# Half of the modulated, transposed features leave PSUM through VectorE

## The chip, the cores and the metric

The kernel runs on one core of one Trainium2 chip. Its time is the device time of one execution in microseconds (us). A core has a matrix engine (TensorE, PE in the profile, with its weight loads as PEld), VectorE (DVE), ScalarE (ACT), GpSimd (POOL) and SyncE (SP), which issues most of the DMAs. Each engine works through its own queue in order, and the engines wait for each other by semaphores.

## The reference, cut to what matters

One step of a two-layer network runs on 128 context tokens and 256 latent tokens, 1024 features wide, in float32. In each layer a token-mixing part and a SwiGLU part are each entered through a normalisation and a modulation:

```python
def rms_norm(x, g):
    xf = x.astype(jnp.float32)
    y = xf * lax.rsqrt(jnp.mean(xf * xf, axis=-1, keepdims=True) + EPS)
    return (y * g.astype(jnp.float32)).astype(x.dtype)

def modulate(h, shift, scale):
    return h * (1 + scale) + shift

h = modulate(rms_norm(x, g_norm_l[0]), sh1, sc1)      # enters the token mixers
x = x + ga1 * rms_norm(mix, g_norm_l[1])
f = swiglu(modulate(rms_norm(x, g_norm_l[2]), sh2, sc2), w_gu_l, w_down_l)
x = x + ga2 * rms_norm(f, g_norm_l[3])
```

So between a residual update and the next matrix products each token's features are divided by their root mean square, multiplied by one number per feature and shifted by another.

## The kernel before, in words

The 384 tokens are three tiles of 128 (tile 0 context, tiles 1 and 2 latent). `x` holds tokens on partitions. The matrix products want the features on partitions, and every float32 product is done as three products of a high and a low part (`mm3`, L107), so the normalised rows must be transposed, modulated and split into a high part `hT[0]` and a low part `hT[1]`.

`norm_T` (L345) does this for one tile and one half `kh` of the features (four blocks of 128). TensorE transposes the four blocks into one PSUM tile `trp` (L350). ScalarE evicts each block with one activation, `scale * in + bias` with the per-feature columns `Amod` and `Bmod` (L355), into the SBUF tile `xm` (`u`). VectorE then casts `xm` to the high part (L359) and subtracts to get the low part (L360). There are three tiles and two halves, and three places where this function is used, 18 calls in all:

- the token mixers of layer 0, for the feed-forward part of layer 0: tiles 0 and 1 at the schedule's steps `00`, `10`, `01`, `11` (first digit the half, second the tile), tile 2 by `tail` inside `gu_first` (L1238);
- the end of the feed-forward part of layer 0, for the mixers of layer 1: `turn` (L1337) for tile 0, and for tiles 1 and 2 the list `tails`, which `tok_first` (L536) puts between its matrix products;
- the token mixers of layer 1, as in layer 0.

The first normalisation of layer 0 has code of its own (`hT_q`, L479) and is not touched.

The order of the work around these calls is fixed by hand. `SCHEDULE` (L22) is a list of step names for each layer, and the steps are traced inside `tc.manual_schedule(engines=ENGINES)`, under which TensorE, VectorE and ScalarE keep exactly the traced order; the two blocks of the feed-forward part that contain `tail` and `turn` are traced in the same way. The end of the list of layer 0 reads:

```python
"... q1b b2 y1 10 v13 A2 A1 01 A3 b2 b2 11 A4 A3 A1 r2a A2 g2a r2b g2b x2a x2b q2a A2 A1 q2b A1 y2 A3"
```

Layer 1 has there `q1b y1 b2 10 v13 01 b2 b2 A3 11 A2 r2a g2a A1 r2b x2a g2b x2b q2a A4 q2b y2`. Here `y1` and `y2` scale the rows of tiles 1 and 2 by their reciprocal root mean square (VectorE, L1171); `v13` is the last attention product and its eviction (L667, L668); `A` steps cast weights into high and low parts (ScalarE L118, VectorE L119); `b2` are the output projection's products of tile 2 and the addition of the two partial sums (VectorE, L749); `r2`, `g2`, `x2`, `q2` are, for tile 2, the sum of squares of the projection, its product with the gate (L1166), the residual update (L1168) and the sum of squares of the new `x` (ScalarE L321 to L326, VectorE L323). After `y2` the tile's rows `xn` go to `tail`.

In the end of the feed-forward part, `post` (L330) is the residual update of a tile (L333, L335), `norm_x` (L337) its normalisation (L311, L139, L140, L342), `next_w` casts weights of the next layer (L118, L119).

`norm_T` returns the last instruction that evicts and the last that subtracts. `gu_first` hands both to `tc.issue_after`, which queues what is traced later behind the given instruction, on that instruction's engine.

Of the kernel before, what the change touches and what calls it, by code (L numbers as in the profile page):

```python
# [11 lines left out]
AF = mybir.ActivationFunctionType  # L12
ALU = mybir.AluOpType
# [39 lines left out]
def hybrid_step(  # L53
# [8 lines left out]
    V, A, PE, G, SP = nc.vector, nc.scalar, nc.tensor, nc.gpsimd, nc.sync  # L62
# [37 lines left out]
    Amod = cp.tile([128, 2, 2, 2, 8], F32, name="Amod")  # L100
    Bmod = cp.tile([128, 2, 2, 2, 8], F32, name="Bmod")
# [243 lines left out]
    def norm_T(l, which, i, hT, t, kh, ps):  # L345
        s = 0 if i == 0 else 1
        u = tp.tile([128, 512], F32, tag="g2", name="xm", bufs=4)
        for k4 in range(4):
            k = 4 * kh + k4
            PE.transpose(ps[:, k4 * 128:(k4 + 1) * 128], t[:, k * 128:(k + 1) * 128], ident)  # L350
        for k4 in range(4):
            k = 4 * kh + k4
            dst = u[:, k4 * 128:(k4 + 1) * 128]
            src = ps[:, k4 * 128:(k4 + 1) * 128]
            a = A.activation(dst, src, AF.Identity, scale=Amod[:, l, which, s, k:k + 1],  # L355
                             bias=Bmod[:, l, which, s, k:k + 1])
        uv = u.rearrange("p (k t) -> p k t", k=4)
        hv = hT[0][:, kh * 4:(kh + 1) * 4, i * 128:(i + 1) * 128]
        V.tensor_copy(hv, uv)  # L359
        v = V.tensor_tensor(hT[1][:, kh * 4:(kh + 1) * 4, i * 128:(i + 1) * 128], uv, hv.bitcast(F32), ALU.subtract)  # L360
        return a.ins, v.ins
# [7 lines left out]
    def mixers(l, ma, mp, mn, pp, banks, h1T, steps, pairs, tails):  # L369
# [718 lines left out]
        def tile_T(i, t, pool, tag, khs=(0, 1)):  # L1088
            if not h2T:
                h2T.extend(new_hT())  # L1090
            for kh in khs:
                r = norm_T(l, 1, i, h2T, t, kh, pool.tile([128, 512], F32, tag=tag, name="trp"))
            return r
# [88 lines left out]
    def ffn(l, fa, fb, pp, steps, h2T, first, tail):  # L1182
# [154 lines left out]
        def turn(i, kh):  # L1337
            def f(pool, tag):
                if i not in xn:
                    xn[i] = norm_x(i)  # L1340
                norm_T(l + 1, 0, i, nh, xn[i], kh, pool.tile([128, 512], F32, tag=tag, name="trp"))
            return f
# [137 lines left out]
```

## Time and profile before

| | us |
|---|---|
| median of 3 runs | 1000.54 (1000.4 to 1001.1) |
| the profiled execution | 1001.41 |
| its span, from first to last instruction | 999.6 |
| TensorE busy | 966.1 (97%) |
| VectorE busy | 623.3 (62%) |
| ScalarE busy | 466.8 (47%) |

Times inside the trace are counted from the start of the span. The calls of `norm_T` lie at 217 to 245 (layer 0), 515 to 535 (between the layers) and 699 to 726 (layer 1).

```profile
PE   5999999999999999999999999999999999999997
PEclk8999999999999999999999999999999999999999
```

These two lines of the page cut the span into 40 slices of 25 us. The first gives TensorE's busy share in tenths, the second the clock granted to it in tenths of full speed: TensorE is nearly always busy, and in every slice but the first at 90% of full clock or more.

### The profile page before, as it was taken

The numbers are of one execution on the slowest core, as the hardware profiler recorded it, in microseconds if no ns is written. First come the engines' busy times: TensorE is split into PE (matmuls) and PEld (weight loads), VectorE is DVE, ScalarE is ACT, GpSimd is POOL, SyncE is SP. The second block draws the span as 40 slices with busy tenths as digits, with TensorE's granted clock in tenths as the row PEclk, the third lists the DMA queues.
The fourth block names the chain that finished last, engine by engine and source line by source line (L and its number), as shares of the span: only waits on it lengthen the run. The fifth ranks groups of instructions, "written<-read, shape, count | busy, mean of one in ns | idle before, by whom it ended". The sixth has DMA issues, their size and how long they took to land.

```text
span 999.6 us, 16493 instructions
## 1 busy us (share of the span) xinstructions
PE 966.1 (97%) x6537; PEld 838.9 (84%) x6537; DVE 623.3 (62%) x1036; ACT 466.8 (47%) x930; POOL 85.8 (9%) x142
## 2 busy tenths in 40 slices
PE   5999999999999999999999999999999999999997
PEld 3789886668999999999987898766899999999996
DVE  3566657767964979986265757677787533333323
ACT  4545537678533433333266346577873323333322
POOL 0312320000000200000010343000000000000000
PEclk8999999999999999999999999999999999999999
DMA  9958678407873777763033794430575344333001
GB/s 327 314 175 255 207 211 237 150 1 253 277 231 126 265 256 236 252 229 110 22 100 107 189 283 122 110 106 1 191 270 192 127 149 148 127 127 127 22 1 64
DMA packets 128414, 167.30 MB, mean 167 GB/s; under 512 B 15600, under 2 KB 90080, under 8 KB 128336
## 3 DMA queue, kind: packets, MB, share of 16 engines
q1 hardware_dynamic: 122112, 154.00, 48.2%
q0 software_dynamic: 5856, 12.09, 4.4%
q8 instruction: 51, 0.84, 0.4%
q14 instruction: 27, 0.22, 0.1%
q10 hardware_dynamic: 368, 0.16, 0.1%
HBM read 163.51 MB, written 2.70 MB: 166 GB/s over the span
## 4 chain that ended last, share of the span: by engine, by line
PE 84%; ACT 5%; DVE 4%; DMA 3%; issue 2%; SPq 1%; POOL 0%; ACTq 0%; DVEq 0%; POOLq 0%
PE gups L108 11%; PE gups L110 11%; PE gups L109 11%; PE facc L108 6%; PE facc L110 6%; PE facc L109 6%; PE tps L108 3%; PE fps L108 2%; PE tps L110 2%; PE tps L109 2%; PE fps L110 2%; PE fps L109 2%; PE ops L108 2%; PE adap L214 2%; PE ptp L1031 2%
## 5 line engine op out<-in xcount | busy, mean ns | idle before, releaser
L119 DVE TENSOR_TENSOR lo<-raw,hi 128x1024 fp32r<-128x1024 f32 x98 | 119.1, 1221 | 65.9 <-ACT hi L118 62.4
L118 ACT ACTIVATE hi<-raw 128x1024 fp32r<-128x1024 f32 x98 | 103.2, 1058 | 93.5 <-PE facc L110 86.9
L108 PE MATMUL gups<-hT,ring 128*128 128x384 f32 x416 | 141.1, 339 | 0.0
L110 PE MATMUL gups<-hT,ring 128*128 128x384 f32 x416 | 140.6, 338 | 0.0
L109 PE MATMUL gups<-hT,ring 128*128 128x384 f32 x416 | 140.4, 338 | 0.0
L179 DVE SCALAR_TENSOR_TENSOR spare<-araw,scol,spare 128x512 f32<-128x512 f32 x168 | 115.6, 745 | 4.5 <-DMA araw<-in_w_ada_dram 4.5
L108 PE MATMUL facc<-hi,f 128*128 128x512 f32 x240 | 95.8, 399 | 0.0
L110 PE MATMUL facc<-hi,f 128*128 128x512 f32 x240 | 94.7, 394 | 0.0
L109 PE MATMUL facc<-lo,f 128*128 128x512 f32 x240 | 94.6, 394 | 0.0
L108 PEld LDWEIGHTS gups<-hT,ring 128*128 128x128 f32 x416 | 78.1, 188 | 0.9 <-issue 0.2
L109 PEld LDWEIGHTS gups<-hT,ring 128*128 128x128 f32 x416 | 78.1, 188 | 0.3
L110 PEld LDWEIGHTS gups<-hT,ring 128*128 128x128 f32 x416 | 78.1, 188 | 0.0
L108 PE MATMUL gups<-hT,xring 128*128 128x384 f32 x224 | 76.0, 339 | 0.0
L110 PE MATMUL gups<-hT,xring 128*128 128x384 f32 x224 | 75.7, 338 | 0.0
L109 PE MATMUL gups<-hT,xring 128*128 128x384 f32 x224 | 75.6, 338 | 0.0
L108 PE MATMUL tps<-hi,hT 128*128 128x512 f32 (+1 forms) x192 | 68.5, 357 | 2.6 <-DVE hT L486 2.6
L110 PE MATMUL tps<-hi,hT 128*128 128x512 f32 (+1 forms) x192 | 65.2, 339 | 0.0
L109 PE MATMUL tps<-lo,hT 128*128 128x512 f32 (+1 forms) x192 | 65.1, 339 | 0.0
L1209 ACT ACTIVATE ring<-spare 128x1024 fp32r<-128x1024 f32 x26 | 27.6, 1060 | 61.3 <-PE gups L109 35.5
L1209 ACT ACTIVATE ring<-rgu 128x1024 fp32r<-128x1024 f32 x26 | 27.6, 1061 | 60.3 <-PE gups L109 35.4
L1224 DVE TENSOR_TENSOR sg<-sg,gups 128x384 f32<-128x384 f32 x40 | 22.1, 552 | 53.7 <-PE gups L110 53.7
L108 PEld LDWEIGHTS facc<-hi,f 128*128 128x128 f32 x240 | 45.1, 188 | 11.2 <-issue 1.8
(304 smaller groups left out, 2018.2 us busy)
## 6 DMA issues: line engine op xcount, KB each, us to landing
araw<-in_w_ada_dram SPq DMA_DIRECT2D x80, 512.0 KB, 4.8
raw<-in_w_down_dram SPq DMA_DIRECT2D x44, 512.0 KB, 4.6
raw<-in_w_in_dram SPq DMA_DIRECT2D x40, 512.0 KB, 5.9
spare<-in_w_gu_dram SPq DMA_DIRECT2D x20, 1024.0 KB, 5.2
rgu<-in_w_gu_dram SPq DMA_DIRECT2D x20, 1024.0 KB, 5.7
sraw<-in_w_ada_dram SPq DMA_DIRECT2D x16, 512.0 KB, 9.8
raw<-in_w_out_dram SPq DMA_DIRECT2D x8, 512.0 KB, 6.3
G<-row POOLq DMA_DIRECT2D x8, 512.0 KB, 6.1
```

What stands on the lines that cost most here:

```text
L108: PE.matmul(out, lhsT=wh, rhs=xh, start=start, stop=False)
L109: PE.matmul(out, lhsT=wh, rhs=xl, start=False, stop=False)
L110: PE.matmul(out, lhsT=wl, rhs=xh, start=False, stop=stop)
L118: a = A.activation(hi[:, :n], raw, AF.Copy)
L119: v = V.tensor_tensor(lo[:, :n], raw, hi[:, :n].bitcast(F32), ALU.subtract)
L179: V.scalar_tensor_tensor(acc[:, s], raw[:, k2], scol[:, k, s:s + 1], acc[:, s], ALU.mult, ALU.add)
L214: PE.matmul(ps[32 * g:32 * g + 32], lhsT=scol[:, 2 * kk + k2], rhs=raw[:, k2, g * 128:(g + 1) * 128], start=k2 == 0, stop=k2 == 1)
L1031: PE.transpose(pt[:, hd, b * 128:(b + 1) * 128], self.P[:, hd, b * 128:(b + 1) * 128], ident)
L1209: A.activation(hi, rv, AF.Copy)
L1224: V.tensor_tensor(sg, sg, pu, ALU.mult)
```

## The change

In `norm_T` the eviction of the second half (`kh` = 1) of each tile is done by VectorE: one multiplication of all four blocks by the column `Amod`, repeated along the tokens by a broadcast view, from PSUM into `xm`, and one addition of `Bmod`, broadcast likewise, in place. The first half stays on ScalarE. The cast and the subtraction follow as before. The instruction returned as `a` is, for the second half, the addition on VectorE.

```diff
-        for k4 in range(4):
-            k = 4 * kh + k4
-            dst = u[:, k4 * 128:(k4 + 1) * 128]
-            src = ps[:, k4 * 128:(k4 + 1) * 128]
-            a = A.activation(dst, src, AF.Identity, scale=Amod[:, l, which, s, k:k + 1],
-                             bias=Bmod[:, l, which, s, k:k + 1])
         uv = u.rearrange("p (k t) -> p k t", k=4)
+        if kh:
+            am, bm = (t[:, l, which, s, 4:8].unsqueeze(2).broadcast_to([128, 4, 128]) for t in (Amod, Bmod))
+            V.tensor_tensor(uv, ps[:, 0:512].rearrange("p (k t) -> p k t", k=4), am, ALU.mult)
+            a = V.tensor_tensor(uv, uv, bm, ALU.add)
+        else:
+            for k in range(4):
+                a = A.activation(u[:, k * 128:(k + 1) * 128], ps[:, k * 128:(k + 1) * 128], AF.Identity,
+                                 scale=Amod[:, l, which, s, k:k + 1], bias=Bmod[:, l, which, s, k:k + 1])
```

## Rows read from the trace of the kernel before

**Rows 1.** Page: busy us of each engine, share of the span, instructions.
```profile
PE 966.1 (97%) x6537; PEld 838.9 (84%) x6537; DVE 623.3 (62%) x1036; ACT 466.8 (47%) x930; POOL 85.8 (9%) x142
```

**Rows 2.** TensorE's waits: total us, times, longest.
```profile
PE trp L350 <- ACT xm L355: 1.8, 2, 0.9
...
PE trp L350 <- DVE xn L1171: 1.2, 2, 0.7
```

**Rows 3.** Groups by line: busy us, mean ns of one, idle us before.
```profile
L119 DVE TENSOR_TENSOR lo<-raw,hi 128x1024 fp32r<-128x1024 f32 x98 | 119.1, 1221 | 65.9 <-ACT hi L118 62.4 <-DMA raw<-in_w_down_dram 3.0
...
L355 ACT ACTIVATE xm<-trp,Bmod,Amod 128x128 f32<-128x128 f32 x72 | 26.9, 462 | 7.8 <-PE trp L350 7.8
...
L333 DVE TENSOR_TENSOR spare<-facc,G 128x512 f32<-128x512 f32 x12 | 8.1, 684 | 8.5 <-ACT junk L321 8.5
...
L635 DVE TENSOR_TENSOR z<-z,s 128x512 f32<-128x512 f32 x6 | 4.8, 796 | 1.9 <-ACT s L140 1.9
...
L1023 DVE TENSOR_TENSOR P<-P,nm 128x512 f32<-128x512 f32 x2 | 1.4, 691 | 0.1
```

**Rows 4.** Timeline of VectorE, layer 1: start, us, instruction; the second reads the first's output.
```profile
717.86 0.68 DVE L1166 TENSOR_TENSOR oP<-oP,G 128x512 f32<-128x512 f32 x1
718.58 0.75 DVE L1168 SCALAR_TENSOR_TENSOR x<-oP,ss,x 128x512 f32<-128x512 f32 x1
```

**Rows 5.** Timeline of VectorE, layer 0, steps y1 to y2.
```profile
225.58 0.75 DVE L1171 TENSOR_SCALAR oP<-x,ss 128x1024 f32<-128x1024 f32 x1 [1.31 <-ACT ss L326]
226.98 0.43 DVE L359 CAST hT<-xm 128x512 fp32r<-128x512 f32 x1 [0.64 <-ACT xm L355]
...
228.05 0.28 DVE L668 TENSOR_TENSOR hT<-av,hT 128x128 fp32r<-128x128 f32 x1
...
229.49 0.43 DVE L359 CAST hT<-xm 128x512 fp32r<-128x512 f32 x1
...
232.90 0.41 DVE L359 CAST hT<-xm 128x512 fp32r<-128x512 f32 x1
...
239.21 0.75 DVE L1171 TENSOR_SCALAR xn<-x,ss 128x1024 f32<-128x1024 f32 x1 [1.17 <-ACT ss L326]
```

**Rows 6.** Timeline of TensorE, the same stretch of layer 0.
```profile
228.66 0.39 PE L110 MATMUL ops<-hi,hT 128*128 128x512 f32 x1
...
240.01 1.10 PE L350 MATMUL trp<-cst,xn 128*128 128x128 f32 x8 [0.52 <-DVE xn L1171]
```

**Rows 7.** Timeline of VectorE, the same steps of layer 1.
```profile
710.75 0.43 DVE L359 CAST hT<-xm 128x512 fp32r<-128x512 f32 x1 [0.90 <-ACT xm L355]
...
713.01 2.35 DVE L119 TENSOR_TENSOR lo<-raw,hi 128x1024 fp32r<-128x1024 f32 x2
715.28 0.42 DVE L359 CAST hT<-xm 128x512 fp32r<-128x512 f32 x1
...
720.87 0.75 DVE L1171 TENSOR_SCALAR xn<-x,ss 128x1024 f32<-128x1024 f32 x1
```

**Rows 8.** Timeline between the layers, VectorE, and one weight load of TensorE.
```profile
518.98 0.43 DVE L359 CAST hT<-xm 128x512 fp32r<-128x512 f32 x1 [0.24 <-ACT xm L355]
...
521.53 0.88 DVE L342 TENSOR_SCALAR xn<-x,ss 128x512 f32<-128x512 f32 x2 [0.25 <-ACT ss L140]
...
526.21 0.41 DVE L359 CAST hT<-xm 128x512 fp32r<-128x512 f32 x1
...
529.38 0.88 DVE L342 TENSOR_SCALAR xn<-x,ss 128x512 f32<-128x512 f32 x2 [0.83 <-ACT ss L140]
...
529.92 0.42 PEld L350 LDWEIGHTS trp<-cst,xn 128*128 128x128 f32 x4 [0.38 <-DVE xn L342]
```

**Rows 9.** Timeline, layer 0, tile 2 by `tail`: VectorE, TensorE, ScalarE.
```profile
244.11 0.69 DVE L360 TENSOR_TENSOR hT<-xm,hT 128x512 fp32r<-128x512 f32 x1
...
247.03 0.39 PE L110 MATMUL guT<-hi,hT 128*128 128x512 f32 x1
...
249.88 1.05 ACT L1209 ACTIVATE ring<-spare 128x1024 fp32r<-128x1024 f32 x1
```

## The prediction, made before the changed kernel ran

> **What bounds the kernel now.** I read the page first. TensorE is busy 97% of the span [rows 1], so a change of ScalarE or VectorE counts only where TensorE stands still for it or starts to. ScalarE is the idler of the two evicting engines over the whole span (47% against 62%), but that share says nothing about the stage. So next come TensorE's waits [rows 2]: twice it waits 0.9 us for `xm`, the very eviction that is changed, and twice some 0.6 us for the scaled rows `xn` of tile 2, which VectorE writes. Last come the timelines of VectorE in the three stages where `norm_T` runs [rows 5, 7, 8]: what the reader is to see there is which rows have an idle time in brackets before them, and which have none. A row with no bracket follows its predecessor at once, and whatever is put ahead of it on VectorE shifts it by its full length.
>
> **What is removed.** Of the 72 activations L355 (462 ns each, [rows 3]) 36 go, four in each of nine calls, and ScalarE's queue gets shorter by some 1.4 to 1.5 us at each of nine places. This alone is worth time only where TensorE waits for `xm`, 1.8 us in all [rows 2].
>
> **What is added, and its price.** Each of the nine calls gets two VectorE operations on 128x512 elements, a multiplication that reads PSUM and an in-place addition. Nearest rows: L333 has a PSUM source and this size, 684 ns; L1023 has an operand repeated by a broadcast view, as here, 691 ns [rows 3]. The cast waits for the addition and the addition for the multiplication. A dependent row follows 0.04 us behind the end of the one before: L1166 begins at 717.86 and takes 0.68, L1168, which reads it, begins at 718.58 [rows 4]. So the pair p takes 2 x (0.68 + 0.04) = 1.44 us of VectorE's queue. From below: independent rows overlap (an L119 takes 1.22 us [rows 3] and two of them 2.35 [rows 7], so they overlap by 0.09), and if the addition did not have to wait, 2 x (0.68 - 0.08) = 1.20. From above: L635, which also has a broadcast operand, has a mean of 796 ns [rows 3], and 2 x (0.80 + 0.04) = 1.68. I take 1.44, since L1023 is the same operation at the same size; a gain below nothing is excluded, because the work is new to VectorE.
>
> The Trainium skill (VectorE: DVE Perf Modes, section "The TRN2 errata — SBUF-src ops pay a fixed extra latency per instruction") gives a VectorE operation 120 cycles plus one per element from PSUM and 58 plus one per element from SBUF, at 0.96 GHz; worked out as an estimate that is 0.66 and 0.59 us, a pair of 1.33 with the two gaps, and the sum below would be 4.3 instead of 4.8. The rows L333 and L1023 are 4 to 16% longer than that, and they decide.
>
> **Layer 0.** Step `10` (tile 0, second half): VectorE finishes L1171 of 225.58 and then idles 0.64 us until ScalarE has evicted [rows 5]. The multiplication takes that place: it can begin at 225.58 + 0.75 - 0.08 = 226.25 and ends at 226.93, where ScalarE's fourth activation ended just before the cast at 226.98. The PSUM bank that TensorE's next transposes wait for therefore comes free at the same moment, and the 0.9 us wait [rows 2] stays. The addition then pushes everything behind it: the cast goes from 226.98 to 226.25 + 1.44 = 227.69, by 0.71. L668 of 228.05, which ended at 228.33, ends at 229.04, and the product of 228.66 [rows 6], which reads it, starts some 0.4 us late. The cast of step `01` at 229.49 has no idle time shown before it, about a tenth is swallowed there, since ScalarE's eviction ended at the same moment. From there to the cast of step `11` at 232.90 VectorE has no gap, and in front of that cast stands the second pair. So it comes at 0.71 - 0.1 + 1.44 = 2.05 us late. Behind it are L119, L323, L1166, L1168, and each is followed by ScalarE's sum of squares, which itself waits for VectorE, down to L1171 at 239.21. TensorE has waited 0.52 us for exactly this row at 240.01 [rows 6], so the 0.4 us stall is swallowed, and the transposes of tile 2 come at 242.06. Cost: 2.05.
>
> For tile 2 itself the third pair is covered. The low part's L360 [rows 9] ended at 244.80; without 1.4 us of ScalarE ahead and with the pair behind the first half's L360, it ends some 1.1 us later relative to the transposes, and the product of 247.03, the first that reads it, has 2.2 us of room. If that cover went, it would be 1.1 us at most.
>
> **Layer 1.** The same steps, but the cast of step `01` at 710.75 has 0.90 us of idle time before it [rows 7], which swallows the first pair's remaining 0.71. The two L119 at 713.01 stand before step `11` here, the cast at 715.28 has no gap, and the second pair moves it and all behind it, down to L1171 at 720.87, by p. Cost: 1.44.
>
> **Between the layers.** Tile 0's second half: VectorE idled 0.24 us before the cast at 518.98, 0.25 before L342 at 521.53 and 0.83 before L342 at 529.38 [rows 8]. These are waits for ScalarE, which is early now, so they are swallowed with some 0.08 of overlap each: 1.32 + 0.24 = 1.56. Two pairs (tile 0 and tile 1) stand before the second L342. The first already moves the cast of tile 1 at 526.21 by 0.7, and TensorE, which reads its low part, stops for it. The rows of tile 2 come 2 x 1.44 - 1.56 = 1.32 us late, and TensorE's transposes at 529.92 waited for them already [rows 8]. Cost: 1.32. The third pair (tile 2) lies before products that come two us later.
>
> **The sum.** 2.05 + 1.44 + 1.32 = 4.8 us, in general 5p - 2.4, so 3.6 to 6.0 with p from 1.20 to 1.68. No transfer is waited for behind these stages, TensorE goes on in its own order and nothing gives the time back. Against the profiled execution (1001.41, span 999.6) that is 1006.2; the median of the runs is 0.87 lower, 1000.54, so I forecast 1005.3, with 1004.1 to 1006.6 as this case's own range.
>
> **Rivals.** (1) Faster. ScalarE is relieved, and PSUM is read by one instruction instead of four. If VectorE's multiplication at steps `10` ran as soon as the transposes are there, both waits for `xm` would go, and if the pairs' length were hidden behind ScalarE's sums of squares, nothing would be given back: 1000.5 - 1.8 = 998.7. It decides whether `10` finds VectorE free before L1171; for it speaks the 1.31 us that VectorE idles before L1171 [rows 5], against it that `y1` stands ahead of `10` in the traced order in both layers. The Trainium skill (ScalarE: Activation LUTs, section "Rules for kernel authors") says to put additions and multiplications on VectorE and not on ScalarE, and speaks for this rival; by these rows the two engines take about the same for the half tile, and VectorE is the one whose queue is full. (2) No change, 1000.5: the order on VectorE is not binding, because tile 2's chain is set by ScalarE's part. Against it: the rows between 229.49 and 232.90 leave no gap. (3) Slower still. The eviction that `norm_T` returns is on VectorE now, so nothing in the feed-forward part is queued behind tile 2's eviction on ScalarE any more. The weight cast L1209 at 249.88 (1.05 us, [rows 9]) can be issued early, and if it stands in the middle of ScalarE's sums of squares for tile 2, the chain gets longer by up to 1.05 in each layer: 1005.3 + 2.1 = 1007.4.
>
> **How the numbers follow.** Forecast 0.74, rival 1 0.05, rival 2 0.07, rival 3 0.14. The range 1002.8 to 1007.5 takes in the forecast's bounds, most of rival 3, and a forecast of which one stage is swallowed; rivals 1 and 2 are left out. A measurement tells about 0.2%, 2 us, from no change. Slower by more than that: 0.74 + 0.14, less a little for a forecast with two stages swallowed, 0.87; within it 0.07; faster 0.06, where only the most of rival 1 counts.
>
> **What would show it.** Right: 36 L355, two new VectorE rows of 0.68 to 0.70 us in each second half; in layer 0 the cast of step `11` near 235 and tile 2's transposes near 242; TensorE's wait for `xn` L1171 near 1.2 + 2.05 + 1.44, less the stalls of about 0.4 in each layer before it, so about 4; a new wait of TensorE for L668; the wait for `xm` replaced by one of the same size for the multiplication. Wrong: transposes of tile 2 at their old place; a pair shorter than 1.2 us; a step of ScalarE found late on the chain, or TensorE's clock lower in these stages than before.

## The result, and the profile after

The changed kernel takes 1007.9 us (median of 4 runs, 1007.8 to 1010.0), beside 1000.8 of the kernel before on the same chip: a ratio of 1.0072, 95% interval 1.0054 to 1.0090. The direction and the larger part of the forecast hold; the time is 2.6 us over the predicted 1005.3 and 0.4 over the upper end of the range. The profiled execution has 1007.97, with a span of 1006.2 against 999.6. In the kernel after, lines behind the change are shifted by two: the cast is L361, the subtraction L362, ScalarE's eviction L358, the pair L354 and L355, the scaled rows L1173, the weight cast L1211 (L1209 before), and L668 is L670. In the kernels of the experiments some lines are up to five further on, by what was inserted ahead of them.

TensorE's waits after (total us, times, longest), beside [rows 2]; the last line is of the kernel before:

```profile
PE trp L350 <- DVE xn L1173: 4.9, 2, 2.5
...
PE trp L350 <- DVE xm L354: 1.8, 2, 0.9
...
PE ops L110 <- DVE hT L670: 1.0, 4, 0.3
...
PE ops L110 <- DVE hT L668: 0.4, 2, 0.2
```

The wait for the bank that the eviction of `10` frees kept its size, 1.8, and only changed the engine. The wait for tile 2's rows went from 1.2 to 4.9 us, and the wait for L670 came four times instead of two, 1.0 us in all instead of 0.4. VectorE in layer 0, beside [rows 5]:

```profile
225.82 0.68 DVE L354 TENSOR_TENSOR xm<-trp,Amod 128x512 f32<-128x512 f32 x1
226.54 0.69 DVE L355 TENSOR_TENSOR xm<-xm,Bmod 128x512 f32<-128x512 f32 x1
227.27 0.43 DVE L361 CAST hT<-xm 128x512 fp32r<-128x512 f32 x1
...
234.51 0.43 DVE L361 CAST hT<-xm 128x512 fp32r<-128x512 f32 x1
...
238.38 1.41 DVE L1170 SCALAR_TENSOR_TENSOR x<-oP,ss,x 128x512 f32<-128x512 f32 x2 [0.31 <-ACT ss L326]
...
241.24 0.75 DVE L1173 TENSOR_SCALAR xn<-x,ss 128x1024 f32<-128x1024 f32 x1 [1.16 <-ACT ss L326]
```

The pair is as priced: from 225.82 to the cast at 227.27 it is 1.45 us. This execution enters the stage 0.43 us earlier than the one before did, so the cast of step `11`, at 234.51 against 232.90, is 2.04 late (the prediction had 2.05). Up to there nothing is missing. Then L1170, which had no idle time ahead of it, waits for ScalarE. ScalarE in layer 0, and the same place in layer 1:

```profile
236.86 1.06 ACT L1211 ACTIVATE ring<-spare 128x1024 fp32r<-128x1024 f32 x1 [2.79 <-DMA spare<-in_w_gu_dram]
237.83 0.28 ACT L325 ACTIVATE ss<-ss 128x1 f32<-128x1 f32 x1
...
722.25 1.06 ACT L1211 ACTIVATE ring<-spare 128x1024 fp32r<-128x1024 f32 x1 [3.90 <-DMA spare<-in_w_gu_dram]
723.22 0.28 ACT L325 ACTIVATE ss<-ss 128x1 f32<-128x1 f32 x1
```

A weight cast of the feed-forward part now stands in the middle of tile 2's root mean square. In front of it ScalarE idles 2.79 and 3.90 us for the weight's DMA, while what tile 2 needs, two operations of 0.3 and 0.2 us, is queued behind. It is not the cast of 249.88 [rows 9] that the prediction had in mind: that one stays in its place (253.16 after), and the one that moved stood ahead of it in the kernel before,

```profile
246.16 1.05 ACT L1209 ACTIVATE ring<-spare 128x1024 fp32r<-128x1024 f32 x1
```

which the feed-forward part issues behind the block of fixed order. TensorE at the end of the two stages, beside [rows 6], and the granted clock in layer 0 (stretch; us, busy us and instructions of PE, PEld, DVE, ACT and POOL, granted clock, DMA share, GB/s):

```profile
242.13 1.94 PE L350 MATMUL trp<-cst,xn 128*128 128x128 f32 x8 [2.49 <-DVE xn L1173]
...
728.23 1.09 PE L350 MATMUL trp<-cst,xn 128*128 128x128 f32 x8 [2.37 <-DVE xn L1173]
```

```profile
241.00:242.00 1.00, 0.00 (x0) 0.00 (x0) 0.75 (x1) 0.20 (x1) 0.00 (x0) 0.99 1.03 362
242.00:243.00 1.00, 0.86 (x4) 0.90 (x5) 0.00 (x0) 0.00 (x0) 0.00 (x0) 0.50 1.10 353
...
245.00:246.00 1.00, 1.00 (x9) 1.00 (x9) 0.97 (x3) 1.00 (x1) 0.00 (x0) 0.80 1.10 349
246.00:247.00 1.00, 1.00 (x11) 1.00 (x10) 0.96 (x2) 0.99 (x2) 0.00 (x0) 1.00 1.08 340
```

From the stage's begin the transposes are 2.12 + 0.43 = 2.55 us later than before in layer 0. The eight take 1.94 us there and 1.09 in layer 1. Behind the 2.49 us in which TensorE had nothing to do its clock is at the lower of its two levels, 1.2 GHz, until inside 245 to 246; in layer 1, behind 2.37 us, it stays at 2.4 GHz.

**How the stages are compared.** A stage of a layer runs from tile 0's first transposes to the first `gups` product (217.51 to 249.30 and 699.03 to 730.96 before), the one between the layers from the first transposes of the turn to tile 2's (515.41 to 529.92). The table gives how much longer each is than before, in us, in one profiled execution of each kernel; "edge" is explained below. Whole times hold one thing more that the change doesn't touch: in 5 of the 17 profiled executions (marked *) the clock fell near 107 us already, and the first stage began 3.0 to 4.2 us later than before, against -0.4 to +1.5 in the others.

| kernel | layer 0 | between | layer 1 | clock fell in |
|---|---|---|---|---|
| after | 4.03 | 1.04 | 2.29 | layer 0 |
| after, second execution* | 2.10 | 1.03 | 2.68 | - |
| edge kept* | 2.11 | 1.03 | 1.61 | - |
| before without edge* | 0.90 | 0.02 | 3.86 | layer 1 |
| after, weight loaded twice | 2.64 | 1.02 | 1.85 | - |
| edge kept, weight loaded twice | 3.62 | 1.02 | 1.59 | layer 0 |
| tile 0 only* | 0.60 | 0.01 | 0.13 | - |
| tile 1 only | 3.02 | 0.01 | 2.98 | both |
| tile 1 only, second execution | 3.02 | 0.01 | 1.45 | layer 0 |
| tile 1 only, idle filled | 1.45 | 0.01 | 1.45 | - |
| tile 2 only | -0.02 | 0.01 | -0.02 | - |
| after, idle filled | 2.06 | 1.04 | 1.82 | - |
| edge kept, idle filled | 2.06 | 1.04 | 1.60 | - |
| four fused operations, edge kept* | 1.95 | 0.94 | 2.07 | - |

In the kernel after, layer 0's 4.03 are the 2.55 at the transposes and 1.48 behind them, where the clock is low. The three stages sum to 7.36; with the 0.43 by which its first stage began earlier and some 0.4 regained between the stages that is the span's 6.6.

### The profile page after: what moved, and what is told of

Read it like the earlier page. It is cut to its first block, busy times and chain, and to the rows that moved or that the text cites. A ratio compares the mean times of both kernels' runs of the same rounds, so it can differ in the third digit from the quotient of the medians.

```text
span 1006.2 us, 16477 instructions
## 1 busy us (share of the span) xinstructions
PE 968.5 (96%) x6537; PEld 840.4 (84%) x6537; DVE 635.0 (63%) x1054; ACT 455.3 (45%) x894; POOL 84.8 (8%) x142
## 4 chain that ended last, share of the span: by engine, by line
PE 82%; ACT 5%; DVE 5%; DMA 5%; issue 2%; SPq 1%; POOL 0%; ACTq 0%; DVEq 0%; POOLq 0%
PE gups L108 11%; PE gups L110 11%; PE gups L109 11%; PE facc L108 6%; PE facc L110 6%; PE facc L109 6%; PE fps L108 2%; PE tps L108 2%; PE fps L110 2%; PE fps L109 2%; PE tps L109 2%; PE tps L110 2%; PE adap L214 2%; PE ptp L1033 2%; PE sc L1004 2%
## 5 line engine op out<-in xcount | busy, mean ns | idle before, releaser
L1211 ACT ACTIVATE ring<-spare 128x1024 fp32r<-128x1024 f32 x26 | 27.6, 1060 | 67.7 <-PE gups L109 38.4
L1211 ACT ACTIVATE ring<-rgu 128x1024 fp32r<-128x1024 f32 x26 | 27.6, 1060 | 59.8 <-PE gups L109 31.9
```

The source lines that it names most:

```text
L1211: A.activation(hi, rv, AF.Copy)
```

## The experiments

Theory 1 is the prediction's: the pair lengthens VectorE's queue, 4.8 us. Theory 2: the instruction handed on as the last eviction is now on VectorE, so ScalarE's queue has lost its order edge (the rule that the feed-forward part's later work on ScalarE stands behind tile 2's eviction), and the weight cast gets in. Theory 3: TensorE's longer idle time lets its clock fall.

**The order edge, restored and taken away.** The first kernel is the one after, handing on ScalarE's eviction of the first half:

```diff
                 r = norm_T(l, 1, i, h2T, t, kh, pool.tile([128, 512], F32, tag=tag, name="trp"))
-            return r
+                if not kh:
+                    on_a = r[0]
+            return on_a if 0 in khs else r[0], r[1]
```

> The kernel after, but the function that hands the last eviction on returns ScalarE's (first half), so that the feed-forward part is again queued behind tile 2's eviction on ScalarE. Theory 1 (the two-operation chain on VectorE alone costs 4.8) together with theory 2 (the lost order edge lets the weight cast L1211 in among ScalarE's sums of squares, about 0.4 in layer 0 and 0.7 in layer 1): the cast goes back behind the eviction, about 1.1 us faster than the kernel after. Theory 3 (TensorE's clock fell because it stood idle 2.5 us in layer 0): with 2.1 us idle the fall may stay away, then another 1.5 us are gained, 2.6 in all, about 1005.3 against 1000.5 of the kernel before. If the edge is not the cause of the cast's early place, the time is that of the kernel after, 1007.9.

Measured: 1006.4 us (median of six, 1005.6 to 1010.7), beside 1001.2 of the kernel before there, ratio 1.0057 (1.0039 to 1.0074). The weight cast is back behind tile 2's eviction, the stages cost 2.11, 1.03 and 1.61, in sum 4.75, and TensorE's rows are:

```profile
246.34 1.06 PE L350 MATMUL trp<-cst,xn 128*128 128x128 f32 x8 [2.09 <-DVE xn L1175]
...
730.87 1.09 PE L350 MATMUL trp<-cst,xn 128*128 128x128 f32 x8 [1.68 <-DVE xn L1175]
```

In the stages that is the forecast's mechanism alone, at its price. The second kernel is the one before, with the edge dropped and nothing else:

```diff
-            ctx_l.enter_context(tc.issue_after(an))
             ctx_l.enter_context(tc.issue_after(v))
```

> The kernel before, with ScalarE's eviction as it was, but without the order edge on ScalarE's last eviction in the feed-forward part. Theory 2 (the edge matters by itself): the weight cast of 249.88 is issued among tile 2's sums of squares, as in the kernel after, and the two waits of TensorE for xn grow by 0.3 to 0.7 each: 0.6 to 1.2 us slower than before. Rival: the cast's early place needs the gaps that the pairs on VectorE leave on ScalarE; then the time is that of the kernel before within 0.3 us.

Measured: 1008.3 us (1003.7 to 1009.5), ratio 1.0060 (1.0041 to 1.0079), more than either theory had; the three stages of the profiled execution hold 4.78 of it. In layer 1 ScalarE is held up between the two operations of one root mean square, for a DMA, and VectorE 2.43 us behind it:

```profile
720.40 0.30 ACT L325 ACTIVATE ss<-ss 128x1 f32<-128x1 f32 x1 [1.22 <-DVE ss L323]
722.15 1.06 ACT L1209 ACTIVATE ring<-spare 128x1024 fp32r<-128x1024 f32 x1 [1.45 <-DMA spare<-in_w_gu_dram]
723.12 0.19 ACT L326 ACTIVATE ss<-ss 128x1 f32<-128x1 f32 x1
```

```profile
723.33 0.75 DVE L1168 SCALAR_TENSOR_TENSOR x<-oP,ss,x 128x512 f32<-128x512 f32 x1 [2.43 <-ACT ss L326]
```

TensorE's wait for xn there is 3.01 us, 2.3 more than before, and the clock fell behind it (3.86 in the table, of which 1.54 stand behind the transposes). So the edge matters by itself, without any pair on VectorE, and its price can be over the cast's 1.06 us.

**What the early cast costs.** The kernel after was profiled once more:

> The kernel after, profiled once more. Theory 2 (the early weight cast L1211 on ScalarE waits for its weight's DMA, so its price is set by the time at which that lands): L1211 again stands among tile 2's sums of squares with a wait for the DMA, the landing shifts by some tenths from execution to execution, and the stages of layers 0 and 1 cost 2.1 to 3 us each, without the clock's fall, against 2.12 and 1.60 with the edge restored. Theory 3 (the clock falls after 2.5 us of idle time in layer 0): it falls again at 242 and costs 1.5 there; if it stays at 1.00 although TensorE idles 2.4 us or more, an idle time of this size does not decide it alone.

```profile
240.11 1.06 ACT L1211 ACTIVATE ring<-spare 128x1024 fp32r<-128x1024 f32 x1 [2.40 <-DMA spare<-in_w_gu_dram]
...
723.95 1.06 ACT L1211 ACTIVATE ring<-spare 128x1024 fp32r<-128x1024 f32 x1 [4.30 <-DMA spare<-in_w_gu_dram]
724.91 0.28 ACT L325 ACTIVATE ss<-ss 128x1 f32<-128x1 f32 x1
```

The order is the same and the weight lands at another time. In layer 1 three executions with this order (the third is the kernel with filled idle time, below) waited 3.45, 3.90 and 4.30 us for it, and the stage cost 1.82, 2.29 and 2.68: each tenth later at the DMA is a tenth later at the stage's end. In layer 0 the waits were 2.29, 2.40 and 2.79, the costs without the clock's fall 2.06, 2.10 and 2.55, so a weight that lands early enough costs nothing over the 2.11 of the pairs. The wait itself is not the price, for with the edge kept ScalarE idles at this place too, until VectorE's L323 is done (layer 0, layer 1):

```profile
241.57 0.29 ACT L325 ACTIVATE ss<-ss 128x1 f32<-128x1 f32 x1 [2.89 <-DVE ss L323]
...
725.78 0.30 ACT L325 ACTIVATE ss<-ss 128x1 f32<-128x1 f32 x1 [4.12 <-DVE ss L323]
```

There L325 begins 0.24 us after L323. Behind the early cast it begins later than that by 0.30, 0.75 and 1.14 us in layer 1, and the stage costs 0.22, 0.68 and 1.07 over the 1.61 (1.60 filled) without the cast. In layer 0 it is 0.37, 0.48 and 0.87 later, and 0, 0 and 0.44 come through. So what counts is how far the end of the cast, its landing and its own length together, lies behind L323. And theory 3 lost its simple form: 2.77 us of idle time in layer 1 of this execution brought no fall.

Then the load that the cast waits for was issued twice, in the kernel after and in the one with the edge kept:

```diff
                 if b2 % 2:
                     raw = spare[g][:, 0:2048].rearrange("p (k f) -> p k f", k=8)
+                if b2 == 1 and not g:
+                    SP.dma_start(raw, w_gu[l, :, g * FF + 256:g * FF + 512].rearrange("(k p) f -> p k f", p=128))
                 else:
                     raw = fb.tile([128, 8, 256], F32, tag="rgu", name="rgu", bufs=2)
...
                 SP.dma_start(raw, w_gu[l, :, c0:c0 + 256].rearrange("(k p) f -> p k f", p=128))
```

The edit does more than that. The `else` now belongs to the new condition, so every other load of an odd block goes to the two buffers `rgu` and no longer to `spare`. These two kernels therefore change the load's landing and the buffers at once.

> The kernel after, with the 1 MB load that the early weight cast L1211 waits for issued twice in each layer, so that it lands about 3 us later (1 MB at the 350 to 380 GB/s of this stretch). Theory 2 (that landing sets what the early cast costs): L1211's wait grows by about 3 us, and so do the waits of TensorE for xn and the costs of both stages: layer 0 and layer 1 about 5 to 6 us each without any fall of the clock, against 2.1 to 2.7 for the kernel after. Rival (the cast itself, 1.06 us of ScalarE's time, is the price): the stages stay where they are within 0.3.

> The same double load in the kernel with ScalarE's edge restored, where the weight cast stands behind tile 2's eviction, 7 us later. Theory 2: the load has landed by then and nothing waits, the stages stay at 2.1 and 1.6. Rival (a double load costs by itself, through the queue behind it): the stages or the block behind get up to 3 us longer here too.

The first missed. The program's order itself changed: the cast now stands behind the second root mean square. Whether that comes from the second load or from the other buffers isn't shown:

```profile
242.54 0.20 ACT L326 ACTIVATE ss<-ss 128x1 f32<-128x1 f32 x1
244.63 1.06 ACT L1213 ACTIVATE ring<-spare 128x1024 fp32r<-128x1024 f32 x1 [1.89 <-DMA spare<-in_w_gu_dram]
```

TensorE's waits for xn are then 2.08 and 1.69, as with the edge kept; the cast is now ahead of tile 2's eviction and costs 0.53 and 0.24 there. This doesn't test the landing at a fixed place, which the three executions above do; it shows that the place changes with the program, while within one program the price changes with the landing. With the edge kept the edit costs nothing in layer 1 (1.59), and nothing in the blocks behind either stage: from layer 0's stage to the next one the time is that of before within 0.01 us, and behind layer 1's it is 0.12 shorter. In layer 0 the wait is the same 2.09 as without it, but here the clock fell (columns as in the table of the granted clock above):

```profile
243.23 1.15 PE L350 MATMUL trp<-cst,xn 128*128 128x128 f32 x8 [2.09 <-DVE xn L1175]
```

```profile
241.00:243.00 2.00, 0.14 (x2) 0.00 (x0) 0.82 (x2) 1.22 (x4) 0.00 (x0) 1.00 1.08 378
243.00:245.00 2.00, 1.77 (x12) 1.80 (x13) 0.08 (x1) 1.10 (x4) 0.00 (x0) 0.77 1.04 386
245.00:247.00 2.00, 2.00 (x12) 2.00 (x11) 1.53 (x3) 1.97 (x4) 0.00 (x0) 0.50 1.10 352
```

The same wait, 2.09 us, once with the fall and once without: 3.62 against 2.11, 1.51 for the fall.

**The pairs one by one.** The condition of the new branch was narrowed to one tile (`kh and which and i == 0`, and so on; for tile 2 with the edge kept). ScalarE's branch then takes the columns `4 * kh + k`:

```diff
-        if kh:
+        if kh and (which and i == 1):
```

> VectorE evicts the second half of tile 0 only, in the token mixers of both layers; all other evictions on ScalarE, order edge as before. Theory 1: the first pair moves the cast of its step by 0.71, a tenth is swallowed in layer 0 and all in layer 1: tile 2's transposes come 0.6 us later in layer 0 and 0 to 0.1 later in layer 1. Rival (each pair costs its length 1.44 wherever it stands): 1.4 in each layer.

> VectorE evicts the second half of tile 1 only, in the token mixers of both layers; all else as before. Theory 1: VectorE has no gap ahead of this step, the full pair of 1.44 us shows in tile 2's transposes in both layers. Rival (ScalarE's side of tile 2's chain sets it): under 0.7 in each.

> VectorE evicts the second half of tile 2 only, in both feed-forward parts, with the order edge kept on ScalarE. Theory 1 (covered by 2.2 us of room): no stage is later, 0.0 in each layer. Rival (the cover does not hold): up to 1.1 us in each layer between tile 2's transposes and the first product of the block behind.

Single profiles of 1005.2, 1007.7 and 1001.2 us. The stages: 0.60 and 0.13 for tile 0; 1.45 in each layer for tile 1 once the clock's falls are out (the runs below); -0.02 twice for tile 2. All three are as theory 1 had them, and the rivals (1.4 for any pair, under 0.7, up to 1.1) are out. The first two add to 2.05 in layer 0 and 1.58 in layer 1, against 2.11 and 1.61 with all pairs and the edge kept. The pairs between the layers were not run one by one.

The last test of the sum takes another eviction, with the edge kept:

```diff
-            V.tensor_tensor(uv, ps[:, 0:512].rearrange("p (k t) -> p k t", k=4), am, ALU.mult)
-            a = V.tensor_tensor(uv, uv, bm, ALU.add)
+            for k in range(4):
+                a = V.tensor_scalar(uv[:, k], ps[:, k * 128:(k + 1) * 128], Amod[:, l, which, s, 4 + k:5 + k],
+                                    Bmod[:, l, which, s, 4 + k:5 + k], ALU.mult, ALU.add)
```

> ScalarE's edge restored, and VectorE evicts each of the four blocks of a second half by one operation with the two columns as per-partition scalars, in place of the pair on the whole half. Theory 1 (the cost over before is 5p - 2.4 with p the time that the eviction holds VectorE's queue, p = 1.44 giving 4.8): four small operations of 0.25 to 0.30 us, nearest to L668's 0.28 at this size, make p 0.9 to 1.2 and the cost over before 2.1 to 3.6. Rival (the fixed cost of four operations makes p longer than the pair's): p of 1.5 or more, 5 us or more.

```profile
229.84 1.36 DVE L354 TENSOR_SCALAR xm<-trp,Amod,Bmod 128x128 f32<-128x128 f32 x4
231.24 0.43 DVE L361 CAST hT<-xm 128x512 fp32r<-128x512 f32 x1
...
717.57 0.43 DVE L361 CAST hT<-xm 128x512 fp32r<-128x512 f32 x1 [0.90 <-ACT xm L358]
```

```profile
715.33 0.66 PE L350 MATMUL trp<-cst,oP 128*128 128x128 f32 x4 [1.56 <-DVE xm L354]
```

The expected 0.25 to 0.30 each was wrong: one takes 0.40, the four 1.36, and p is 231.24 - 229.84 = 1.40, hardly less than the pair. At that p the sum gives 4.6; the stages cost 4.96 (ratio 1.0051, 1.0033 to 1.0069). Layer 0's 1.95 is the 2p - 0.83 of the prediction, 1.97. Layer 1's 2.07 is over its 1.40, because all four operations read PSUM: the bank comes free later, TensorE waits 1.56 us for it instead of 0.89, ScalarE's eviction of the next half follows later, and VectorE's cast of step `01` stands 0.90 us idle instead of 0.17. With so small a step in p this is no test of the slope.

**The idle time, filled.** Sixteen transposes of the identity into tile 2's bank, overwritten by the real ones, stand ahead of them:

```diff
+        if which and i == 2 and not kh:
+            for _ in range(16):
+                PE.transpose(ps[:, 0:128], ident, ident)
         for k4 in range(4):
```

> The kernel after with sixteen additional transposes of the identity into tile 2's bank in each layer, ahead of its real ones; they fill TensorE's 2.4 us of idle time and their result is overwritten. Theory 3 (the clock fell to half because TensorE stood idle): the granted clock stays at 1.00 at 242 to 246 in layer 0, the eight transposes take 1.1 instead of 1.94 us, and the time falls by about 1.5 us against the kernel after, 1006.4; layer 1, which kept its clock, stays as it is or loses 0.1. Rival (the clock's fall comes from something else, by chance at this place): the clock falls all the same and the time is 1007.9 or more.

> The same sixteen transposes put into the kernel with ScalarE's edge restored. Theories 1 to 3 together: only the pair chain is left, 4.8 us over the kernel before, 1005.3. If restoring the edge already keeps the clock, it equals the kernel with the edge restored within 0.3 us; if the clock falls there, it is 1.5 us faster than that.

> VectorE evicts the second half of tile 1 only, once more, timed. Theory 3 (an idle stretch of TensorE of about 2.1 us lets the clock fall in some executions, at 1.5 us each): 2 x 1.45 = 2.9 us over before in executions without a fall, 4.4 with one and 5.9 with two, so the times spread over about 3 us. Rival (the clock has nothing to do with the stage): 2.9 and no fall near 242 and 727.

> The same with sixteen additional transposes of the identity ahead of tile 2's in each layer, which fill the idle stretch and are overwritten. Theory 3: the clock stays at 1.00 in both stages, each costs 1.5 (as without a fall), 2.9 to 3.1 over before, and the time's spread at these places goes. Rival (the falls are not brought by the idle stretch): the granted clock falls to half near 242 or 727 here too.

The kernel after, filled, had 1006.34 in its profiled execution, with the clock at 2.4 GHz in both stages, but 1006.3 to 1013.3 over six (median 1009.7, ratio 1.0081, 1.0060 to 1.0102), so the fill doesn't make this kernel faster; where the slow ones lost it, no profile shows. With the edge kept it is 1006.5 (ratio 1.0057, 1.0042 to 1.0072), the same as unfilled. With tile 1 alone, beside a kernel before that spread over 1000.6 to 1005.2 there: unfilled 1007.6 (1004.8 to 1008.8), ratio 1.0040 (1.0024 to 1.0055); filled 1005.0 (three of nine from 1003.8 to 1003.9, and up to 1007.5; a tenth run of 3318 us stands apart), ratio 1.0025 (1.0012 to 1.0038). The intervals overlap. The stages are clearer. TensorE and the granted clock in layer 0, unfilled (second execution), and filled:

```profile
241.66 1.06 PE L350 MATMUL trp<-cst,xn 128*128 128x128 f32 x8 [2.08 <-DVE xn L1174]
```

```profile
243.00:245.00 2.00, 2.00 (x12) 2.00 (x11) 1.10 (x2) 2.00 (x7) 0.00 (x0) 0.50 1.10 347
```

```profile
239.23 1.91 PE L350 MATMUL trp<-cst 128*128 128x128 f32 x16
241.37 1.09 PE L353 MATMUL trp<-cst,xn 128*128 128x128 f32 x8 [0.24 <-DVE xn L1177]
```

```profile
243.00:245.00 2.00, 2.00 (x19) 2.00 (x18) 1.12 (x2) 1.98 (x7) 0.00 (x0) 1.00 1.10 347
```

Over the kernels of the table, before included: TensorE waited 2.08 us or more for xn in 13 stages, and in 6 of them the clock fell; it waited 1.83 or less in 11, and 6 were filled, and in none of these 17 did it fall. So in these kernels the fall went with the longer wait, and what decides in one of those 13 stays open. That the fill keeps the clock up is likely and not shown: 6 stages without a fall are few beside 6 falls in 13. A fall costs 1.48 to 1.57 us.

**Another order.** The profile of before suggests to move what TensorE does between its two waits for xm. Layer 0 of the first order (layer 1 alike), and of the second:

```diff
- q1b b2 y1 10 v13 A2 A1 01 A3 b2 b2 11 A4 A3 A1 r2a A2 g2a r2b g2b x2a x2b q2a A2 A1 q2b A1 y2 A3
+ q1b b2 y1 v13 10 A2 A1 b2 b2 01 A3 11 A4 A3 A1 r2a A2 g2a r2b g2b x2a x2b q2a A2 A1 q2b A1 y2 A3
+ q1b b2 y1 v13 10 A2 b2 b2 A1 01 A3 r2a r2b 11 g2a g2b x2a x2b q2a q2b A4 A3 A1 y2 A3
```

> The kernel before with another order of the last steps: the last attention product (v13) ahead of step 10, and tile 2's projection (b2 b2) between 10 and 01, in both layers. If TensorE's two waits for xm (0.9 each) go and tile 2's rows are not later, up to 1.8 us are gained, 998.9; if tile 2's chain on ScalarE and VectorE is what ends last, as theory 1 has it, what is gained ahead of it is lost at tile 2's transposes: 0 to 0.4.

> As the other reordered kernel, and tile 2's sums of squares (r2a, r2b) ahead of tile 1's second half (11), weight casts behind them. Theory 1 (tile 2's chain ends last): moving its steps forward gains where the reorder of the matrix products alone doesn't, 1.2 to 3.0 us over both layers, 997.5 to 999.3. Rival: tile 1's high and low parts come too late for the first product that reads its second half, and TensorE waits there instead: no gain or 1 us slower.

Measured: 1005.6 (one of ten, at 1907 us, stands apart), ratio 1.0034 (1.0021 to 1.0047), and 1010.8, ratio 1.0088 (1.0070 to 1.0105). Both lose, and the first in a way that neither theory had. Its waits:

```profile
PE gu L108 <- DVE hT L359: 1.7, 2, 1.3
PE trp L350 <- DVE oP L749: 1.5, 2, 1.3
```

The transposes of step `11` now wait for the bank that L749 frees, and the products behind them for the high part. The waits for xm and xn are gone, 3.0 us, and 3.2 of others have come; the clock fell in both layers (at 232 and 716), also behind these shorter waits, and the stages cost 2.35 and 2.29. The second order has the same two lines, waits for xn again (0.96 and 2.15), and its clock fell in both layers and once more near 607, far from the change; its stages cost 3.63 and 4.67. Its rival had the direction, 0 to 1 us, and not the size. No kernel here beats the one before. An order with `10` ahead of `y1`, on which rival 1 rests, was not run.

## Where the prediction was right, and where it failed

- **The price of the pair and its place** were right: 0.68 and 0.69 us, 1.45 with the gaps, against 1.44. The estimates from the table of the Trainium skill (VectorE: DVE Perf Modes, "The TRN2 errata — SBUF-src ops pay a fixed extra latency per instruction"), 0.66 and 0.59, were 0.02 and 0.10 too low here; below its table the same section gives 0.691 us for a float32 addition of 512 elements, and that is what the addition took.
- **The terms.** Layer 0: 2.05 predicted, 2.11 with the edge kept. Layer 1: 1.44 against 1.61; the addition L751 waits for the product that L670 had delayed (1.44 us for two instead of 1.28), 0.16 that I had swallowed. Between the layers: 1.32 against 1.03; the second L342 begins 1.16 later, and TensorE's transposes follow its begin after 0.42 us instead of 0.54. In sum 4.8 against 4.75 in the stages; the medians of the whole time differ by 5.2 (1006.4 against 1001.2).
- **Tile 2's pair is covered**: -0.02 in both layers. The additional wait for L668 and the unchanged wait for the bank came as said.
- **The step that failed** is "nothing gives the time back" taken as "nothing is added": the sum went from the pairs straight to the span and put two terms at nothing, ScalarE's part of tile 2's chain and TensorE's clock. The runs show 4.75 for the pairs, 1.12 for the first term and 1.48 for the second, together the 7.36 of the stages within 0.01.
- **The first term** is rival 3, which was not a rival to the forecast but an addition to it. Its mechanism was named (the lost edge, a weight cast in ScalarE's sums of squares, the chance 0.14), for the wrong one of the casts, and the cast was early in every profiled execution without the edge except where the edit of the load had moved its place. In the kernel after it cost 0.44 in layer 0 (2.55 against 2.11) and 0.68 in layer 1, within rival 3's "up to 1.05 in each layer". That bound is the cast's own length and doesn't hold in general, since a late landing is added to it: 1.07 in layer 1 of the second execution, and 2.3 in layer 1 of the kernel before without the edge (0.9 in layer 0).
- **The clock** was named as what would make the prediction wrong and had no price in the sum. In the profiled execution it is 1.48 of the 7.36. Whether it falls changes from execution to execution (the second had no fall in these stages), so that it fell in the profiled one is luck, as far as these runs show.
- **Rivals 1 and 2** are out: `10` finds VectorE busy with L1173, so that the multiplication ends no earlier than ScalarE's eviction did (TensorE waits 0.89 us for the bank, 0.90 before), and tile 2's chain does hang on VectorE. The rule of the Trainium skill (ScalarE: Activation LUTs, "Rules for kernel authors") that spoke for rival 1 doesn't ask which queue the chain runs through; here the same half tile takes 1.5 us on ScalarE and 1.45 on VectorE, and the nine of them cost 4.75 for standing in VectorE's queue.

## What to carry to other kernels

A change of engine moves an instruction out of one queue and out of every order that hung on it: look for what is returned, and who is queued behind it. An instruction that waits for a DMA blocks its engine's queue for the whole of that wait, so price it by how far its end, the landing and its own length together, lies behind the moment at which the next one would have been ready. And where TensorE's wait for a chain gets longer, its clock is a term of its own in the sum.

## What was not expected of the hardware

Behind a wait of TensorE of 2.08 to 3.01 us its clock fell from 2.4 to 1.2 GHz in 6 of 13 cases, at 1.48 to 1.57 us each, and the same wait of 2.09 us in the same place did and did not bring it. In the first reordered kernel it fell behind waits of 1.33 us and less. A VectorE operation with two per-partition scalars from PSUM took 0.40 us on 128x128, where the operation with two tensors took 0.68 on 128x512: a quarter of the elements, and over half of the time.
